# Hybrid attention block on one core: keys and values of units 4 to 15 as seven products of quarters, and head results kept in device memory until their gates

## The chip, the cores and the metric

The kernel runs on one core of a Trainium2 chip. The core has five engines, each with a queue of its own that it works through in order: PE (TensorE, matrix products), DVE (VectorE), ACT (ScalarE), POOL (GpSimd) and SP (SyncE, which here only issues DMAs). Engines wait for each other through semaphores. The metric is the device time of one execution in microseconds; 734.61 is the median of three runs before the change (734.28 to 734.91).

## What is computed

One decoder block on 512 tokens with 16 meta tokens in front (528 rows), 1024 channels, all in float32. Eight differential heads and sixteen stick-breaking heads, each branch with a SiLU gate:

```python
h = layer_norm(concat([meta, x]), emb_ln_g, emb_ln_b)             # 528 x 1024
q_d,k_d,v_d,g_d, q_s,k_s,v_s,g_s, m_d,m_s = split(h @ w_in)       # 10 x 1024 columns
a   = softmax(q1 k1' + alibi) - lam * softmax(q2 k2' + alibi)     # differential, 8 heads
y_d = rms_norm(a @ v_d, diff_subln_g) * (1 - lam_init)
y_s = stick_breaking(q_s, k_s) @ v_s                              # 16 heads
br_d = (y_d * silu(g_d)) @ w_br_diff
br_s = (y_s * silu(g_s)) @ w_br_sb
merged = sigmoid(m_d + b0) * br_d + sigmoid(m_s + b1) * br_s
out = layer_norm(DN_ALPHA * h + merged @ w_out, ln_g, ln_b)[16:]
```

## The kernel before

**Three passes.** h stands transposed in SBUF, channels on partitions, as eight k-tiles of 128 channels by 528 columns. It is held as a rounded part `hTh` and the rest `hTl` (L348), and every weight tile is split in the same way: `wh` by a cast on ACT (L153), `wl` by a subtraction on DVE (L158). A product is wh·hTh + wh·hTl + wl·hTh, three matmuls per k-tile.

**Weights.** They come as halves of four k-tiles (128 x 4 x 128, 256 KB). `items` and `loads` (L83 to L99) list them in the order of use; `fetch` (L118) issues the loads on SP into a ring `raw` of six, and `prep(h)` (L162) casts and splits half h and goes on fetching. It is called four halves ahead of the product that uses it. Where an item is a pair, `add` (L135) forms the sum of two halves on DVE, and where a load has a second source, POOL issues a DMA that adds it to the first in SBUF (L129).

**Units.** `UNITS` holds eight differential heads (kind d), then eight pairs of stick-breaking heads (kind s). Iteration u of the main loop runs the attention of unit u in steps between the projections of later units: keys (`stage_k`, L540) and values (`stage_v`, L567) of unit u+1, the query (`stage_q`, L527) of unit u+2, and, in s units, the two gates of that pair index. Keys and values run in `proj_pos` (L453): 8 k-tiles x 3 passes x 2 halves of 264 columns, 48 matmuls each, 96 a unit (L462). Query and gates run in `proj_tok` (L439): 24 matmuls of 512 columns. `stage_k` splits its result into `ks` (ACT L555, DVE L556), and `store_k` (L559) copies it into the one K buffer of each head by SP DMAs, as a step at 9.2 in the middle of the iteration; `stage_v` copies its result into `vT` on ACT (L574). `values` (L577) transposes vT on PE (tv, L582; the 16 meta rows t4, L586). PSUM has three banks for projections (`pj`).

**Order.** `run` interleaves the projection generators with attention steps at given times, and a scheduler then orders the middle of the program on each engine by its own estimate. `keep_order` (L192) pins the order of the start only. Everything between may move.

**Results.** d heads end in `ydT[:, h, :]` (L748), s pairs in `ysT`, two tiles of 16 KB a partition that live until the gates have been multiplied in (`gate`, L470, on POOL) and the branch products read them.

**Late stage.** The branch products already use seven products of quarters instead of eight (`pair`, L872, L886, 256 columns), on sums of quarters formed by `operands` (L853) and of weight quarters.

## Time and profile before

| what | value |
|---|---|
| median of three runs | 734.61 us (734.28 to 734.91) |
| profiled execution | 734.92 us |
| its span | 733.1 us, 13328 instructions |
| mean granted clock of PE | 0.994 |
| PE, DVE, ACT, POOL busy | 719.2, 529.9, 411.1, 176.6 us |
| DMA moved | 84.03 MB, mean 115 GB/s |

A group of instructions in the profile reads: line, engine, operation, output<-inputs, sizes, count | busy us in all, mean ns of one | idle us of the engine ahead of them and what ended it. A row of the timeline reads: start us, duration us, engine, line, operation, and in brackets the idle time before it with the instruction that ended it. Matmuls overlap in the array: one of 264 columns is listed with 0.28 us, while the next starts earlier.

### The profile page before, as it was taken

The numbers are of one execution on the slowest core, as the hardware profiler recorded it, in microseconds if no ns is written. First come the engines' busy times: TensorE is split into PE (matmuls) and PEld (weight loads), VectorE is DVE, ScalarE is ACT, GpSimd is POOL, SyncE is SP. The second block draws the span as 40 slices with busy tenths as digits, with TensorE's granted clock in tenths as the row PEclk, the third lists the DMA queues.
The fourth block names the chain that finished last, engine by engine and source line by source line (L and its number), as shares of the span: only waits on it lengthen the run. The fifth ranks groups of instructions, "written<-read, shape, count | busy, mean of one in ns | idle before, by whom it ended". The sixth has DMA issues, their size and how long they took to land.

```text
span 733.1 us, 13328 instructions
## 1 busy us (share of the span) xinstructions
PE 719.2 (98%) x4690; PEld 659.4 (90%) x4690; DVE 529.9 (72%) x1098; ACT 411.1 (56%) x987; POOL 176.6 (24%) x241
## 2 busy tenths in 40 slices
PE   8999999999999999999999999999999999999994
PEld 7999999999999989898989898988888998999883
DVE  6776667666766688585858585858385878788887
ACT  5675667566756756564646464646364456555300
POOL 3232244224412213120303030313022201230002
PEclk9999999999999999999999999999999999999997
DMA  9153443334323334232323333332248837696902
GB/s 292 37 145 101 104 117 91 89 99 117 93 83 102 95 95 113 77 104 75 106 81 100 90 95 94 89 88 71 73 114 156 170 109 185 135 185 186 313 17 101
DMA packets 134788, 84.03 MB, mean 115 GB/s; under 512 B 6161, under 2 KB 128434, under 8 KB 134722
## 3 DMA queue, kind: packets, MB, share of 16 engines
q1 hardware_dynamic: 125090, 76.36, 36.4%
q0 software_dynamic: 9312, 5.77, 5.9%
q10 hardware_dynamic: 320, 1.06, 0.4%
q8 instruction: 37, 0.61, 0.3%
q14 instruction: 29, 0.24, 0.1%
HBM read 67.32 MB, written 2.10 MB: 95 GB/s over the span
## 4 chain that ended last, share of the span: by engine, by line
PE 88%; DVE 6%; DMA 3%; POOL 1%; issue 1%; ACT 1%; SPq 0%; POOLq 0%; ACTq 0%; DVEq 0%
PE ps L462 25%; PE ps L448 12%; PE ps L446 11%; PE ps L447 11%; PE q L886 10%; PE sc L615 6%; PE t L621 4%; PE t L626 1%; DMA lgb<-in_ln_b_dram 1%; PE bank L337 1%; PE av L783 1%; PE tv L582 1%; PE av L784 1%; DVE hr L1035 1%; DMA raw<-in_w_out_dram 1%
## 5 line engine op out<-in xcount | busy, mean ns | idle before, releaser
L158 DVE TENSOR_TENSOR wl<-raw,wh 128x512 fp32r<-128x512 f32 x180 | 125.5, 704 | 93.9 <-ACT wh L153 85.8
L153 ACT CAST wh<-raw 128x512 fp32r<-128x512 f32 x180 | 110.8, 622 | 75.3 <-PE ps L447 62.0
L462 PE MATMUL ps<-hTh,wh 128*128 128x264 f32 x512 | 146.9, 287 | 0.0
L462 PE MATMUL ps<-hTl,wh 128*128 128x264 f32 x512 | 146.5, 286 | 0.0
L462 PE MATMUL ps<-hTh,wl 128*128 128x264 f32 x512 | 146.4, 286 | 0.0
L447 PE MATMUL ps<-hTl,wh 128*128 128x512 f32 x368 | 145.0, 394 | 0.0
L448 PE MATMUL ps<-hTh,wl 128*128 128x512 f32 x368 | 144.7, 393 | 0.0
L446 PE MATMUL ps<-hTh,wh 128*128 128x512 f32 x368 | 144.4, 393 | 0.0
L462 PEld LDWEIGHTS ps<-hTh,wh 128*128 128x128 f32 x512 | 96.5, 188 | 1.0
L462 PEld LDWEIGHTS ps<-hTl,wh 128*128 128x128 f32 x512 | 96.5, 188 | 1.0
L462 PEld LDWEIGHTS ps<-hTh,wl 128*128 128x128 f32 x512 | 96.5, 189 | 0.3
L448 PEld LDWEIGHTS ps<-hTh,wl 128*128 128x128 f32 x368 | 69.2, 188 | 13.1
L446 PEld LDWEIGHTS ps<-hTh,wh 128*128 128x128 f32 x368 | 69.2, 188 | 13.0
L447 PEld LDWEIGHTS ps<-hTl,wh 128*128 128x128 f32 x368 | 69.2, 188 | 12.5
L615 PE MATMUL sc<-k,A 128*128 128x264 f32 (+3 forms) x320 | 68.5, 298 | 0.2 <-POOL k L525 0.2
L769 DVE TENSOR_TENSOR_SCAN e<-e,after 128x528 f32<-128x528 f32 (+1 forms) x64 | 55.9, 883 | 13.2 <-ACT e L761 12.8
L886 PE MATMUL q<-gh,wh 128*128 128x256 f32 x224 | 63.5, 283 | 0.2 <-ACT t L895 0.2
L767 POOL TENSOR_SCALAR_AFFINE_SELECT e<-e 128x128 f32<-128x128 f32 x64 | 38.7, 612 | 103.3 <-ACT e L763 94.6
L886 PE MATMUL q<-gl,wh 128*128 128x256 f32 x224 | 63.4, 283 | 0.0
L886 PE MATMUL q<-gh,wl 128*128 128x256 f32 x224 | 63.4, 283 | 0.0
L707 POOL TENSOR_SCALAR e<-e,rz 128x528 f32<-128x528 f32 (+3 forms) x32 | 38.4, 1200 | 100.2 <-DVE rz L706 100.2
L631 ACT CAST ah<-t 128x512 fp32r<-128x512 f32 (+2 forms) x88 | 39.4, 464 | 37.0 <-PE t L621 30.6
(239 smaller groups left out, 1419.2 us busy)
## 6 DMA issues: line engine op xcount, KB each, us to landing
raw<-in_w_in_dram SPq DMA_DIRECT2D x152, 256.0 KB, 3.0
k<-ks SPq DMA_DIRECT2D x60, 132.0 KB, 2.6
raw<-in_w_out_dram SPq DMA_DIRECT2D x16, 256.0 KB, 3.3
k<-ks SPq DMA_DIRECT2D x60, 66.0 KB, 2.0
raw<-in_w_br_diff_dram SPq DMA_DIRECT2D x12, 256.0 KB, 3.0
raw<-in_w_br_sb_dram SPq DMA_DIRECT2D x12, 256.0 KB, 3.7
raw<-in_w_in_dram SPq DMA_DIRECT2D x4, 512.0 KB, 6.2
rawa<-in_w_br_diff_dram SPq DMA_DIRECT2D x8, 256.0 KB, 4.5
```

The costliest lines, as they stand in the source:

```text
L153: s.copy(wh, raw)
L158: eng.tensor_tensor(wl, raw, wh.bitcast(F32), op=ALU.subtract)
L446: pe.matmul(ps, wh[:, k % 4, :], hTh[:, k, M:], start=(k == 0), stop=False)
L447: pe.matmul(ps, wh[:, k % 4, :], hTl[:, k, M:], start=False, stop=False)
L448: pe.matmul(ps, wl[:, k % 4, :], hTh[:, k, M:], start=False, stop=(k == KT - 1))
L462: pe.matmul(ps[:, :H2], a[:, k % 4, :], b[:, k, ts(c, H2)], start=(k == 0 and m == 0), stop=(k == KT - 1 and m == 2))
L615: pe.matmul(ps[:, :n], q, K[:, m, k0:k0 + n], start=(m == 0), stop=(m == 1))
L631: s.copy(h, t[:, o:o + w])
L707: g.tensor_scalar(e[0], e[0], r[:, 0:1], None, op0=ALU.mult)
L767: g.affine_select(own, own, pattern=[[-1, P]], compare_op=ALU.is_gt, fill=0.0, base=0, channel_multiplier=1)
L769: v.tensor_tensor_scan(rev, rev, after[0][:, L - nk:][:, ::-1], 1.0, ALU.mult, ALU.max)
L886: pe.matmul(bank, a[:, k, :], b[:, n, k, :], start=start and k == 0 and m == 0, stop=k == 3 and m == 2, skip_group_check=not start)
```

## The change

From unit 4 on (`SEVEN = 4`, 12 of 16 units), `stage_kv` takes the place of `stage_k` and `stage_v`. It sees keys and values as one product of 2 x 2 quarters: weights by (key or value) and (first or last four k-tiles), h by (first or last four k-tiles) and (positions 0 to 263 or 264 to 527). Strassen's scheme in Winograd's form gives the four result quarters from seven products of 12 matmuls (4 k-tiles x 3 passes), 84 a unit. The line numbers from here on are those of the changed kernel.

It needs sums of weight quarters: per unit two of the five loads get a second source by an accumulating DMA of POOL (ring `rawk` of 4), and two more sums are formed by `add` on DVE. There are seven items a unit to cast and split, where there were four halves. It also needs four sums of quarters of h, made once: `input_sums(k)` for four pairs of k-tiles, into `tS` (rounded) and four tiles `tl` (rest). For that the float h (`hF`) is kept in pair tiles, its 16 meta columns apart in `hM`. Since the `tS` and `tl` tiles take the room of `ysT` and `ydT`, the results wait in device memory: a d head's `yd` is stored there (L827), an s unit loads it back for its gate, `gate` stores both gated results (L493), and the last unit reloads them. `store_k` is called at the end of `stage_kv` instead of by a step. The ring of sums has one buffer instead of two.

```diff
+SEVEN = 4
...
-            seq += [(x + UNITS[u + 1][0], UNITS[u + 1][1]) for x in "kv"]
+            other, i = UNITS[u + 1]
+            seq += [(x + other, i) for x in ("w" if u + 1 >= SEVEN else "kv")]
...
-            loads += [(a11, None), (a21, a11), (a21, a22), (a12, None), (a22, None)]
+            loads += [(a11, None, "raw"), (a21, a11, ring), (a21, a22, ring), (a12, None, "raw"), (a22, None, "raw")]
...
-    rings = {False: ("raw", 6, []), True: ("rawa", 4, [])}
+    rings = {"raw": (6, []), "rawk": (4, []), "rawa": (4, [])}
...
-    hF = ypool.tile([P, KT, L], F32, tag="yd", name="hF")
+    hP = [pair_of("hF") for k in range(4)]
+    hF = [hP[k % 4][:, k // 4, :] for k in range(KT)]
+    hM = const.tile([P, KT, M], F32, name="hM")
...
-        g.tensor_tensor(y[:, j, :], sg, y[:, j, :], op=ALU.mult)
+        y = y()
+        g.tensor_tensor(y, sg, y, op=ALU.mult)
+        if store is not None:
+            nc.sync.dma_start(store, y)
...
+        def input_sums(k):
+            g.tensor_copy(hP[k][:, :, :M], hM[:, k:k + 5:4])
+            b11, b12, b21, b22 = [hP[k][:, m, ts(n, H2)] for m in range(2) for n in range(2)]
+            v.tensor_tensor(b22, b12, b22, op=ALU.subtract)
+            v.tensor_tensor(b12, b11, b12, op=ALU.subtract)
+            v.tensor_tensor(b11, b22, b11, op=ALU.subtract)
+            v.tensor_tensor(b21, b11, b21, op=ALU.add)
+            h, l = tS[0][:, k:k + 5:4], pair_of("tl", F32R)
+            s.copy(h, hP[k])
+            v.tensor_tensor(l, hP[k], h.bitcast(F32), op=ALU.subtract)
+            tL.append(l)
+
+        def stage_kv(unit, kind, n):
+            i = take("w" + kind, n, 7)
+            x, z, y = [pj.tile([P, 512], F32, tag="pj", name="q")[:, :H2] for m in range(3)]
...
+            yield from product(0, x, 0)
+            s.copy(u, x)
+            yield from product(1, z, 5)
+            s.copy(z7, z)
+            yield from product(2, x, 4, False)
+            s.copy(w, x)
+            yield from product(3, y, 1)
+            v.tensor_tensor(u, y, u, op=ALU.add)
+            keys(0, u)
+            yield from product(4, x, 3, False)
+            v.tensor_tensor(vT[:, H2:], z7, x, op=ALU.subtract)
+            yield from product(5, z, 6, False)
+            v.tensor_tensor(vT[:, :H2], z, w, op=ALU.subtract)
+            unit["vT"] = vT
+            yield from product(6, x, 2, False)
+            keys(1, x)
+            store_k()
...
-            v.scalar_tensor_tensor(ydT[:, h, :], av, g08, r, op0=ALU.mult, op1=ALU.mult)
+            y = gpool.tile([P, S], F32, tag="sg", name="yd")
+            v.scalar_tensor_tensor(y, av, g08, r, op0=ALU.mult, op1=ALU.mult)
+            nc.sync.dma_start(kept["d"][h], y)
...
         def keys_values(unit, kind, n):
+            if UNITS.index((kind, n)) >= SEVEN:
+                return [stage_kv(unit, kind, n)]
             return [stage_k(unit, kind, n), stage_v(unit, kind, n)]
...
-            if not last:
-                steps.append((10.6 if kind == 's' and n == 0 else 9.2, store_k))
+            if u + 1 < SEVEN:
+                steps.append((9.2, store_k))
+            if u + 4 in (SEVEN + 1, SEVEN + 2):
...
+                for m in range(2):
+                    steps.append((5.0 + 6.0 * m, lambda k=2 * (u + 3 - SEVEN) + m: input_sums(k)))
...
                 if last:
...
+                    nc.sync.dma_start(ydT[7], kept["d"][7])
+                    for y, of in ((ydT, "gd"), (ysT, "gs")):
+                        for j in range(7):
+                            nc.sync.dma_start(y[j], kept[of][j])
...
+                    yd, unit["y"] = [gpool.tile([P, S], F32, tag="sg", name=x) for x in ("yd", "ys")]
+                    nc.sync.dma_start(yd, kept["d"][n])
+                    proj += [gate("d", n, lambda yd=yd: yd, kept["gd"][n]),
+                             gate("s", n, lambda unit=unit: unit["y"], kept["gs"][n])]
```

`input_sums` is written as steps of iterations u = 1 and u = 2. Where the scheduler puts it shows on DVE in the opening, between the copies of unit 0's second half of K (`ps_453`, `ps_484`) and the first low weight half of unit 1 (`wl_520`). Before, DVE has this there:

```order
L551 TENSOR_TENSOR k1_450<-ps_453,k1_450 64x264
L312 SCALAR_TENSOR_TENSOR A0_172<-bank_181,A0_172 64x512
L312 SCALAR_TENSOR_TENSOR A1_173<-bank_181,A1_173 64x512
L551 TENSOR_TENSOR k0_449<-ps_484,k0_449 64x264
L551 TENSOR_TENSOR k1_450<-ps_484,k1_450 64x264
L698 ISA e0_447,mn_618<-sc_621,bias_612 128x264
L698 ISA mn_618 128x1
L158 TENSOR_TENSOR wl_520<-raw_119,wh_519 128x512
```

After the change, in the stretch that ends with the same half (`wl_550`; the banks are `ps_483` and `ps_514`), it reads:

```order
L568 TENSOR_TENSOR k1_456<-ps_483,k1_456 64x264
L602 TENSOR_TENSOR hF_177<-hF_177 128x264
L602 TENSOR_TENSOR hF_178<-hF_178 128x264
L602 TENSOR_TENSOR hF_179<-hF_179 128x264
L605 TENSOR_TENSOR tl_1094<-hF_176,tS_956 128x1056
L319 SCALAR_TENSOR_TENSOR A0_174<-bank_187,A0_174 64x512
L319 SCALAR_TENSOR_TENSOR A1_175<-bank_187,A1_175 64x512
L568 TENSOR_TENSOR k0_455<-ps_514,k0_455 64x264
L605 TENSOR_TENSOR tl_1222<-hF_177,tS_956 128x1056
L605 TENSOR_TENSOR tl_1453<-hF_178,tS_956 128x1056
L568 TENSOR_TENSOR k1_456<-ps_514,k1_456 64x264
L605 TENSOR_TENSOR tl_1573<-hF_179,tS_956 128x1056
```

All four `input_sums` have moved up into the opening; the other thirteen of their sixteen 128x264 operations stand above these rows, among the first copies of K, and behind them come one score and `wl_550`. On ACT the casts into `tS` (L604) stand between the copies of K in the same stretch, ahead of `wh_549`, the high half that goes with it:

```order
L567 CAST k0_455<-ps_514 64x264
L604 CAST tS_956<-hF_177 128x2x528
L604 CAST tS_956<-hF_178 128x2x528
L604 CAST tS_956<-hF_179 128x2x528
L569 CAST k0_455<-ps_514 64x264
L567 CAST k1_456<-ps_514 64x264
L569 CAST k1_456<-ps_514 64x264
L160 CAST wh_549<-raw_121 128x512
```

Before, the four copies of that half of K (L550 and L552) stand there one behind the other with `wh_519` next; only the three casts are new among them.

The second place is PE in a d unit, around the transposition t4 of the meta rows of the unit's own values. Before:

```order
L725 MATMUL av_2546<-al0_2494,V_2274 128x512
L726 MATMUL av_2546<-ah0_2493,V_2274 128x512
L586 MATMUL t4_2604<-idents_127,vT_2382 16x128
L615 MATMUL sc_2703<-k0_449,A0_2238 128x272 x2
L462 MATMUL ps_2712<-hTh_148,wh_2479 128x264
L462 MATMUL ps_2712<-hTl_149,wh_2479 128x264
```

After, at the corresponding transposition (`q_2683` is the bank x of `stage_kv`):

```order
L802 MATMUL av_2656<-al0_2609,V_2373 128x512
L803 MATMUL av_2656<-ah0_2608,V_2373 128x512
L663 MATMUL t4_2715<-idents_129,vT_2345 16x128
L692 MATMUL sc_2852<-k1_456,A1_2337 128x272 x2
L692 MATMUL sc_2867<-k0_455,A0_2336 128x144 x2
L626 MATMUL q_2683<-hTh_150,wh_2770 128x264
```

The 24 matmuls of the query projection (`ps_2933`, L459 to L461) now stand ahead of these rows, with ten matmuls on `av` between; the seventh product, which adds to bank x after DVE has read that bank for vT, is now the last projection of the unit. Before, key and value matmuls stood behind t4 and the query projection followed them. On DVE that read (L646) stands here, behind the query's A0 and one `apad`:

```order
L165 TENSOR_TENSOR wl_3029<-rawk_2505,wh_3028 128x512
L552 SCALAR_TENSOR_TENSOR A0_3018<-ps_2933,A0_3018 64x512
L786 SCALAR_TENSOR_TENSOR apad0_433<-e1_454,rz_2698,e0_453 128x400
L646 TENSOR_TENSOR vT_2686<-kvt_1662,q_2683 128x264
L648 TENSOR_TENSOR vT_2686<-q_2684,kvt_1662 128x264
```

Before, vT was written by a copy of ACT (L574), and no matmul of the keys and values waited for it.

105 lines of the change are left out of this document (71 added, 34 removed).

## The prediction

> **What bounds the kernel now.** The page's shares of the span, the granted clock in 40 slices and the chain that ended last are read first.
>
> ```profile
> PE 719.2 (98%) x4690; PEld 659.4 (90%) x4690; DVE 529.9 (72%) x1098; ACT 411.1 (56%) x987; POOL 176.6 (24%) x241
> ...
> PEclk9999999999999999999999999999999999999997
> ...
> PE 88%; DVE 6%; DMA 3%; POOL 1%; issue 1%; ACT 1%; SPq 0%; POOLq 0%; ACTq 0%; DVEq 0%
> PE ps L462 25%; PE ps L448 12%; PE ps L446 11%; PE ps L447 11%; PE q L886 10%; PE sc L615 6%; PE t L621 4%; PE t L626 1%; DMA lgb<-in_ln_b_dram 1%; PE bank L337 1%; PE av L783 1%; PE tv L582 1%; PE av L784 1%; DVE hr L1035 1%; DMA raw<-in_w_out_dram 1%
> ```
>
> TensorE is busy 98% of 733.1 us at an undiminished clock, and a quarter of the chain is L462, the keys and values that the change rewrites. The view of waits, for TensorE, holds nothing but this:
>
> ```profile
> PE warm L267 <- POOL idents masks.py:199: 1.5, 1, 1.5
> PE bank L300 <- DVE xn L296: 0.9, 1, 0.9
> PE bank L300 <- ACT cols L362: 0.2, 1, 0.2
> PE q L886 <- ACT t L895: 0.2, 1, 0.2
> PE sc L615 <- POOL k L525: 0.2, 1, 0.2
> ```
>
> That is 3.0 us in all, 2.6 of it in the opening. From the first unit on TensorE waits for nobody, so a matmul taken out there is worth its full spacing until some other engine comes late. How near the others are, the windows show (start:end, length, then busy time with count of PE, PEld, DVE, ACT, POOL, then clock, DMA share, GB/s).
>
> ```profile
> 29.20:38.60 9.40, 9.24 (x76) 9.03 (x75) 4.96 (x11) 4.70 (x12) 7.01 (x19) 1.00 0.01 3
> ...
> 102.45:126.81 24.36, 24.36 (x176) 23.07 (x174) 16.50 (x48) 16.06 (x43) 9.10 (x11) 1.00 0.40 107
> ...
> 255.00:289.00 34.00, 34.00 (x232) 31.55 (x231) 31.16 (x52) 22.39 (x61) 10.47 (x14) 1.00 0.34 93
> ...
> 420.25:436.00 15.75, 15.75 (x131) 15.73 (x130) 13.30 (x22) 11.51 (x32) 6.34 (x8) 1.00 0.27 79
> 436.00:457.50 21.50, 21.50 (x111) 18.19 (x111) 12.63 (x26) 9.53 (x22) 1.91 (x3) 1.00 0.37 103
> ```
>
> A differential unit lasts 24.36 us with VectorE busy 16.50. A stick-breaking unit lasts 37.25 us: 15.75 of keys and values with VectorE at 84%, then 21.50 of query and gates with VectorE at 59%. From 255 to 289 VectorE is 92% busy and TensorE still loses nothing.
>
> **What is saved.** Each of the 12 changed units runs 7 products of 12 matmuls, 84, where L462 ran 96: 12 fewer a unit, 144 in all, with the same 264 columns. Their spacing is read from start to start:
>
> ```profile
> 33.57 0.29 PE L462 MATMUL ps<-hTl,wh 128*128 128x264 f32 x1
> 33.69 0.28 PE L462 MATMUL ps<-hTh,wl 128*128 128x264 f32 x1
> 33.81 0.28 PE L462 MATMUL ps<-hTh,wh 128*128 128x264 f32 x1
> ```
>
> 0.12 us (0.28 is the pipelined length). L462's share of the chain gives the same: 25% of 733.1 over 1536 matmuls is 0.119. At a median spacing of 0.121, 144 are 17.4 us, or 1.45 us a unit. [...] The seven-product scheme already runs in the late stage (L886), where the only wait is the 0.2 us above, so the scheme in itself starves nothing.
>
> **What it costs at the start.** The scheduler has placed all four `input_sums` into the opening, ahead of the low weight halves of unit 1. That is 16 VectorE operations of 128x264, four of 128x1056, and four ScalarE casts of 128x1056. The nearest rows:
>
> ```profile
> L348 DVE TENSOR_TENSOR hTl<-hF,hTh 128x256 fp32r<-128x256 f32 x16 | 5.6, 418 | 0.0
> L868 DVE TENSOR_TENSOR gl<-t,gh 128x1024 fp32r<-128x1024 f32 x8 | 9.8, 1226 | 1.5 <-ACT gh L867 1.5
> L867 ACT CAST gh<-t 128x1024 fp32r<-128x1024 f32 x8 | 8.4, 1055 | 13.0 <-DVE t L864 13.0
> ...
> 25.00 2.77 DVE L348 TENSOR_TENSOR hTl<-hF,hTh 128x256 fp32r<-128x256 f32 x8
> ```
>
> Eight subtractions of 256 columns in 2.77 us are 0.346 apiece; times 264/256 that is 0.357, and 16 take 5.7 us. A 128x1056 takes 1.226 x 1056/1024 = 1.26 alone, some 1.2 in a row; four take 4.8. Together **10.5 us of VectorE**. What room is there? Between 29.2 and 38.6 VectorE is busy 4.96 of 9.40 us (window above): 4.4 idle, all of it waiting for ScalarE's copies.
>
> ```profile
> 34.54 1.39 DVE L312 SCALAR_TENSOR_TENSOR A<-bank,A 64x512 fp32r<-64x512 f32 x2 [1.66 <-ACT A L307]
> ...
> 38.63 1.90 DVE L158 TENSOR_TENSOR wl<-raw,wh 128x512 fp32r<-128x512 f32 x3 [0.49 <-ACT wh L153]
> ...
> 39.94 0.28 PE L462 MATMUL ps<-hTh,wl 128*128 128x264 f32 x1
> ```
>
> The first wl is ready at 38.63 + 0.69 = 39.3 and used at 39.94, a slack of 0.6. So 10.5 - 4.4 - 0.6 = 5.5. Walking the copies, sums and casts in their new order, with ScalarE's casts of 1.05 standing between the copies of K, the first key matmul that needs wl starts at 45.5 instead of 39.94: **5.6 us**. Full durations instead of spacings give 7.6; the low end is 0, if the scores and values can be moved so that TensorE has work meanwhile, but its row holds only unit 0's 48 value matmuls (5.8 us) before them, as before. Nothing later gives this back, since TensorE is the bound afterwards. GpSimd can add to it:
>
> ```profile
> 150.02 1.64 POOL L683 TENSOR_SCALAR bias<-bias 128x528 f32<-128x528 f32 x1 [0.46 <-DVE mn L698]
> ...
> 150.18 1.11 DVE L158 TENSOR_TENSOR wl<-raw,wh 128x512 fp32r<-128x512 f32 x1
> ```
>
> A wl of 0.69 takes 1.11 us beside a 1.64 us bias on POOL; two such biases run in the opening, so up to 0.8 more, which I keep in the upper end. [...]
>
> **What it costs in the differential units** (five of them work on units 5 to 9 of the 16). Prices:
>
> ```profile
> L158 DVE TENSOR_TENSOR wl<-raw,wh 128x512 fp32r<-128x512 f32 x180 | 125.5, 704 | 93.9 <-ACT wh L153 85.8 <-PE av L785 6.9
> L153 ACT CAST wh<-raw 128x512 fp32r<-128x512 f32 x180 | 110.8, 622 | 75.3 <-PE ps L447 62.0 <-PE ps L462 10.4 <-PE q L886 1.6
> L535 DVE SCALAR_TENSOR_TENSOR A<-ps,A 64x512 fp32r<-64x512 f32 x28 | 19.3, 688 | 1.9 <-ACT A L534 1.1
> L534 ACT ACTIVATE A<-ps 64x512 fp32r<-64x512 f32 x28 | 16.6, 592 | 4.4 <-DVE A L535 3.6
> L556 DVE TENSOR_TENSOR ks<-ps,ks 128x264 fp32r<-128x264 f32 x30 | 12.8, 426 | 3.6 <-ACT ks L555 3.3
> L140 DVE TENSOR_TENSOR sum<-rawa,raw 128x512 f32<-128x512 f32 x8 | 5.5, 684 | 0.0
> L709 DVE SCALAR_TENSOR_TENSOR apad<-e,rz,e 128x400 f32<-128x400 f32 x8 | 5.8, 728 | 0.0
> ...
> 175.53 0.39 PE L446 MATMUL ps<-hTh,wh 128*128 128x512 f32 x1
> ...
> 178.28 0.39 PE L446 MATMUL ps<-hTh,wh 128*128 128x512 f32 x1
> ```
>
> Seven weight halves instead of four are 3 x 0.70, two sums 2 x 0.68, and u, and the two vT halves that leave ScalarE, 3 x 0.43: 4.75 us more VectorE a unit, 21.25 of 22.9 us (24.36 - 1.45), or 93%. ScalarE gains three casts of 0.6 and about one copy, some 2.2 us, of a third that is idle. The share says it fits; the order says where it doesn't. The last product adds to the bank from which vT (L646) is read, so TensorE waits for that read. Behind the last query matmul VectorE's row has A0 (after ScalarE's A), apad 128x400, then vT: 0.39 (the matmul's end behind its start) + 0.59 + 0.69 + 0.73 + 0.43 = 2.8, some 2.6 with VectorE's overlap of successive operations. TensorE has ten matmuls on `av`, t4 and two pairs of scores in that time: 3328 + 128 + 832 columns at 0.447 ns (twelve of 512 columns start in the 2.75 us from 175.53 to 178.28, 0.229 each), with the query matmul's own 0.23, 2.1 us. That leaves 0.5 us a unit, **2.7 us** over five (2.5 by this sum, rounded up for a queue at 93%); the ends are 0, if the query's A comes earlier, and 1.2 each.
>
> **What it costs in the stick-breaking units** (seven). 4.75 us on 25.9 gives 30.7 of 35.8, 86%. Within the 14.3 us that remain of the keys and values 13.30 + 4.75 would be too much, but the order has part of the products stand among the query and gate matmuls, where VectorE has 8.9 us idle. Walked waits keep 1.3 to 1.5 us of slack; I take 0.17 each, **1.2 us**, with ends 0 and 3.75 each (18.05 - 14.3).
>
> **What is hidden.** The results kept in device memory and reloaded are loads of 256 KB under a DMA share of 0.4 or less; POOL's two accumulating loads a unit occupy a quarter-used engine.
>
> ```profile
> rawa<-in_w_br_diff_dram SPq DMA_DIRECT2D x8, 256.0 KB, 4.5
> rawa<-in_w_br_diff_dram POOLq DMA_DIRECT2D x8, 256.0 KB, 6.2
> k<-ks SPq DMA_DIRECT2D x60, 132.0 KB, 2.6
> ```
>
> An accumulation lands 6.2 us after its issue, behind a 4.5 us plain load; the ring of four is fetched a whole unit ahead, so I cost it at nothing. If that cover failed, a unit would lose up to 6.2. SP waits a few microseconds where a result isn't finished; six buffered weight halves hold some 16 us of TensorE's work. The last unit's 15 reloads wait on the release of the operands tS and tl, with gates in between: nothing. K's second half is stored right behind the last product, and has about 0.4 us to spare on a landing of 2.6.
>
> **The sum**, against the profiled execution's 734.92 (span 733.1 and 1.8 around it; the median shown is 734.61): 734.9 - 17.4 + 5.6 + 2.7 + 1.2 = **727.0 us**. A measurement of this kernel can tell about 0.2% from no change, so faster is below 733.1 and slower above 736.1.
>
> **The rivals.** (a) *The covers hold*: the opening overlaps and VectorE keeps up. For it: TensorE lost nothing at 92% VectorE. Against it: the order at the start. 734.9 - 17.4 = 717.5, with a stall or two 718. (b) *Slower: VectorE becomes the bound of the stick-breaking units' keys and values.* If nothing moved into the gates' time, 3.75 x 7 = 26 us on top of the 5.6 and 2.7: 752; with half of it, 741. It decides from a loss of 17.4/12 = 1.45 us a unit, opening included. Against it: the order does spread the products. (c) *K's halves land late*, 0.5 to 1.2 us in 12 units: 727 + 6 to 14, 733 to 741, near no change. For it: 0.4 us of slack; against it: stores of 2.6 us were never waited for before. (d) *A clock drop after the opening's stall*: the trace shows the clock at 1.00 in the opening window, but also no gap there as long as the 3 us now to come. Were half the clock granted for some 4 us behind it, 2 to 3 us of work would be lost: 730. [...]
>
> **How the numbers follow.** Forecast (725 to 731) 0.50; (a) 0.18; (b) 0.13; (c) 0.12; (d) 0.07. Its own range follows from 5.6 to 7.6 at the start, 0 to 1.2 in five units and 0 to 0.3 in seven. The range that leaves out (b) alone, and a little of (c), goes from 717 to 737. Faster: 0.50 + 0.18 + 0.07 + part of (c), 0.80; same 0.06; slower, (b) and the rest of (c), 0.14.
>
> **What would show it.** L626 with 1008 matmuls at 0.12 spacing and 384 left to the old line confirms the saving. The first key matmul of unit 1 near 45.5, behind VectorE's hF and tl rows, confirms the opening; near 40 refutes it. Waits of TensorE on vT L646, five of about 0.5, confirm the differential units; waits on wl or sums of over a microsecond in the stick-breaking units mean (b), on k<-ks (c), a PEclk digit under 9 in the second slice or third (d). The forecast is wrong if VectorE's order under load makes one late operation queue behind the next, so that stalls add up unit by unit.

## The result, and the profile after

| | before | after |
|---|---|---|
| median, beside each other on one chip | 734.76 us (734.28 to 736.24, 4 runs) | 746.78 us (745.65 to 747.76, 4 runs) |
| profiled span | 733.1 us | 744.7 us |
| mean granted clock of PE | 0.994 | 0.983 |

The ratio is 1.016, with a 95% interval of 1.0138 to 1.0181: the changed kernel is **slower by 12.0 us**, where 727.0 was forecast, and it lies outside the range. The page of the changed kernel first: busy shares, granted clock in 40 slices, the chain by engine.

```profile
PE 716.7 (96%) x4546; PEld 651.2 (87%) x4546; DVE 597.4 (80%) x1214; ACT 441.2 (59%) x1043; POOL 212.3 (29%) x269
...
PEclk9989999999999998999999999999999999999998
...
PE 80%; DVE 7%; DMA 4%; POOL 3%; issue 3%; ACT 3%; SPq 0%; ACTq 0%; DVEq 0%; POOLq 0%
```

TensorE runs 144 matmuls less (4690 to 4546), as forecast, but its share of the chain falls from 88% to 80%, and POOL, which had 1%, now has 3%. Two slices have an 8 in the clock where there was a 9. The view of waits says for whom TensorE waits (us in all, times, longest):

```profile
PE q L626 <- DVE vT L646: 6.1, 4, 2.4
PE av L863 <- DVE al L709: 3.6, 1, 3.6
PE ps L475 <- ACT k L569: 2.5, 1, 2.5
PE sc L692 <- ACT e L842: 2.3, 1, 2.3
...
PE sc L692 <- POOL k L542: 1.2, 1, 1.2
...
PE sc L692 <- DMA k<-ks: 0.2, 1, 0.2
```

Where they lie, the windows show (start:end, length, then busy time with count of PE, PEld, DVE, ACT, POOL, then clock, DMA share, GB/s). First the changed kernel:

```profile
20.00:40.00 20.00, 16.30 (x114) 15.37 (x113) 19.47 (x54) 13.18 (x34) 9.08 (x26) 0.91 0.36 79
...
100.00:240.00 140.00, 133.26 (x907) 124.08 (x906) 115.74 (x297) 98.09 (x254) 63.20 (x70) 0.99 0.58 135
240.00:300.00 60.00, 53.21 (x322) 47.68 (x321) 45.51 (x78) 44.04 (x99) 19.32 (x26) 0.91 0.48 121
...
380.00:540.00 160.00, 159.87 (x958) 141.71 (x958) 129.13 (x228) 95.83 (x240) 35.05 (x45) 1.00 0.49 139
```

The same stretches of the kernel before:

```profile
100.00:240.00 140.00, 140.00 (x993) 132.48 (x993) 93.93 (x256) 92.14 (x240) 47.27 (x65) 1.00 0.36 97
240.00:300.00 60.00, 60.00 (x383) 54.29 (x382) 46.06 (x80) 38.95 (x95) 13.18 (x18) 1.00 0.35 98
```

There TensorE was busy throughout. Now it is idle for 3.7 us in the opening, for 6.7 in the differential units and for 6.8 at the passage to the stick-breaking units; from 300 us on it loses next to nothing.

The same loss by spacing: I take the time from a matmul's start to the next one's start, subtract the median for its size, and add up what is over 0.15 us. Beside it stands what the matmuls lose while the clock is at one half (left out: the first 20 us, where the first 128x128 matmuls of both kernels stand 0.21 us apart, up to 4.2 us before and 5.7 after, and the next ones 0.11).

| stretch, us | before | after: stalls | after: half clock |
|---|---|---|---|
| 20 to 60 (opening) | 0.5 | 4.5 | 2.5 |
| 60 to 240 (differential units) | 0.0 | 7.7 | 1.6 |
| 240 to 300 (passage) | 0.0 | 9.4 | 3.8 |
| 300 to the end | 0.4 | 1.4 | 0 |

That is 23.0 + 7.9 us lost, against 0.9 before; less the 17.4 saved it makes 12.6, where the spans differ by 11.6. Some 1.4 us stand in both columns: at the passage, matmuls of 512 columns that the clock slows lose over 0.15 us each and count as stalls too.

The saving itself is there. The groups of TensorE by form (count, then busy us and mean ns of one):

```profile
L626 PE MATMUL q<-tS,wh 128*128 128x264 f32 x192 | 56.0, 292 | 0.8 <-DVE A L552 0.7
...
L626 PE MATMUL q<-hTh,wh 128*128 128x264 f32 x144 | 42.8, 297 | 6.1 <-DVE vT L646 6.1
...
L475 PE MATMUL ps<-hTh,wh 128*128 128x264 f32 x128 | 38.3, 299 | 2.5 <-ACT k L569 2.5
```

Three forms of 192 and three of 144 are 1008 matmuls on L626, and 3 x 128 = 384 stay on the old line, as forecast.

**One stall followed back.** The timeline of the changed kernel around the first long wait on vT, POOL, VectorE and TensorE one below the other (start, duration; in brackets the idle time before and what ended it):

```profile
178.56 1.28 POOL L136 DMA_DIRECT2D rawk<-in_w_in_dram  x1 [5.45 <-DMA rawk<-in_w_in_dram]
179.35 2.14 POOL L784 TENSOR_SCALAR e<-e,rz 128x528 f32<-128x528 f32 x1
180.94 0.72 POOL L785 TENSOR_TENSOR rz<-rz,nlam 128x1 f32<-128x1 f32 x1
...
176.06 0.16 DVE L783 RECIPROCAL rz<-zs 128x2 f32<-128x2 f32 x1
...
181.69 0.77 DVE L786 SCALAR_TENSOR_TENSOR apad<-e,rz,e 128x528 f32<-128x528 f32 x1 [2.43 <-POOL rz L785]
...
185.49 0.43 DVE L646 TENSOR_TENSOR vT<-kvt,q 128x264 f32<-128x264 f32 x1
...
185.97 0.39 PE L626 MATMUL q<-hTh,wh 128*128 128x264 f32 x1 [2.40 <-DVE vT L646]
```

POOL had the accumulating load next in its queue and waited 5.45 us for the plain load that it adds to. The reciprocal that the scaling of e (L784) needs was ready at 176.22, but L784 stands behind that DMA and starts at 179.35. So VectorE waits 2.43 us for rz, forms apad late, comes to A and then to vT late, and TensorE waits 2.40 us. The forecast had half a microsecond at this place.

### The profile page after: what moved, and what is told of

It reads as the page before. It is cut to its first block, busy times and chain, and to the rows that moved or that the text cites. A ratio compares the mean times of both kernels' runs of the same rounds, so it can differ in the third digit from the quotient of the medians.

```text
span 744.7 us, 13453 instructions
## 1 busy us (share of the span) xinstructions
PE 716.7 (96%) x4546; PEld 651.2 (87%) x4546; DVE 597.4 (80%) x1214; ACT 441.2 (59%) x1043; POOL 212.3 (29%) x269
## 4 chain that ended last, share of the span: by engine, by line
PE 80%; DVE 7%; DMA 4%; POOL 3%; issue 3%; ACT 3%; SPq 0%; ACTq 0%; DVEq 0%; POOLq 0%
PE q L626 15%; PE ps L460 11%; PE ps L459 11%; PE ps L461 11%; PE q L985 9%; PE ps L475 6%; PE sc L692 5%; PE t L698 3%; DMA lgb<-in_ln_b_dram 1%; PE t L703 1%; DMA rawk<-in_w_in_dram 1%; PE bank L350 1%; PE av L862 1%; PE av L863 1%; POOL e L784 1%
## 5 line engine op out<-in xcount | busy, mean ns | idle before, releaser
L459 PE MATMUL ps<-hTh,wh 128*128 128x512 f32 x368 | 145.8, 396 | 0.0
L461 PE MATMUL ps<-hTh,wl 128*128 128x512 f32 x368 | 145.3, 395 | 0.0
L160 ACT CAST wh<-raw 128x512 fp32r<-128x512 f32 x168 | 102.9, 621 | 35.5 <-PE ps L460 20.6
L461 PEld LDWEIGHTS ps<-hTh,wl 128*128 128x128 f32 x368 | 69.6, 189 | 12.9
L459 PEld LDWEIGHTS ps<-hTh,wh 128*128 128x128 f32 x368 | 69.6, 189 | 12.8
L460 PEld LDWEIGHTS ps<-hTl,wh 128*128 128x128 f32 x368 | 69.6, 189 | 12.1
L784 POOL TENSOR_SCALAR e<-e,rz 128x528 f32<-128x528 f32 (+3 forms) x32 | 46.1, 1441 | 56.9 <-DVE rz L783 56.9
L136 POOL DMA_DIRECT2D rawk<-in_w_in_dram x24 | 32.4, 1381 | 99.5 <-DMA rawk<-in_w_in_dram 62.2
L709 DVE TENSOR_TENSOR al<-t,ah 128x512 fp32r<-128x512 f32 (+2 forms) x88 | 45.7, 525 | 18.4 <-ACT ah L708 11.2
L692 PEld LDWEIGHTS sc<-k,A 128*128 128x128 f32 x320 | 51.4, 192 | 9.2 <-ACT e L842 2.7
L626 PE MATMUL q<-tS,wh 128*128 128x264 f32 x192 | 56.0, 292 | 0.8 <-DVE A L552 0.7
L626 PE MATMUL q<-tl,wh 128*128 128x264 f32 x192 | 55.4, 289 | 0.0
L626 PE MATMUL q<-tS,wl 128*128 128x264 f32 x192 | 55.0, 288 | 0.0
```

The source lines that it names most:

```text
L160: s.copy(wh, raw)
L459: pe.matmul(ps, wh[:, k % 4, :], hTh[:, k, M:], start=(k == 0), stop=False)
L460: pe.matmul(ps, wh[:, k % 4, :], hTl[:, k, M:], start=False, stop=False)
L461: pe.matmul(ps, wl[:, k % 4, :], hTh[:, k, M:], start=False, stop=(k == KT - 1))
L626: pe.matmul(bank, a[:, k, :], b, start=start and k == 0 and j == 0, stop=k == 3 and j == 2, skip_group_check=not start)
L692: pe.matmul(ps[:, :n], q, K[:, m, k0:k0 + n], start=(m == 0), stop=(m == 1))
```

## The experiments

Each time stands beside the kernel before on the same chip.

| run | what it is | median us | ratio to before (95%) |
|---|---|---|---|
| e1_sums | after, sums of the input out of the opening | 740.79 | 1.008 (1.006 to 1.011) |
| e5_park | results parked in device memory, no seven products | 736.82 | 1.002 (1.000 to 1.004) |
| e9_noacc | e1 without the accumulating loads | 728.69 | 0.991 (0.990 to 0.993) |
| e8_noadd | e1 without VectorE's weight sums | 732.95 | 0.997 (0.995 to 0.999) |
| e10_both | e1 without either | 728.64 | 0.989 (0.986 to 0.992) |
| e2_pool | after, accumulations issued three halves later | 760.68 | 1.036 (1.034 to 1.038) |
| e11_window | e1, accumulations at a fixed step | 750.96 | 1.020 (1.017 to 1.023) |
| e13_early | e1, accumulations a unit earlier | 741.04 | 1.007 (1.005 to 1.010) |
| e12_junk | e9 and 24 accumulations into spare memory | 741.91 | 1.009 (1.006 to 1.013) |
| e14_plain | e9 and 24 copies by SP | 729.49 | 0.992 (0.990 to 0.994) |
| e17_work | e9 and 24 x 1.3 us of POOL's time | 728.93 | 0.991 (0.989 to 0.992) |
| e19_pinned | e1 in e9's order | 749.78 | 1.022 (1.019 to 1.025) |
| e3_tables | after, ScalarE's table loads grouped | 753.56 | 1.025 (1.022 to 1.027) |
| e4_all | e1, e2 and e3 together | 757.76 | 1.032 (1.030 to 1.034) |
| e7_s9 | seven products from unit 9 on | 734.70 | 0.999 (0.998 to 1.000) |
| e15_s11 | from unit 11 on, table loads grouped | 728.56 | 0.990 (0.989 to 0.992) |
| e16_s11n | from unit 11 on | 728.50 | 0.991 (0.989 to 0.992) |
| e18_s10 | from unit 10 on | 727.49 | 0.989 (0.987 to 0.991) |

### The opening, and the results in device memory

`place()` ties an instruction behind the one that was written before it on the same engine, so that the scheduler can't draw the sums into the opening.

```diff
             v.tensor_tensor(b22, b12, b22, op=ALU.subtract)
+            place()
             v.tensor_tensor(b12, b11, b12, op=ALU.subtract)
+            place()
```

> One edit to the changed kernel: the first two VectorE operations of each input_sums are ordered behind the VectorE instruction that the program issues before them, so that the sums stay in iterations 1 and 2 instead of the opening. If the opening's loss comes from them (the ms matmul of unit 0 stands 6.9 us later than before, that of unit 1 6.3), they start within 1 us of before and the time falls by about 6 us to some 741. Rival: the 10.5 us of VectorE only move into units that are nearly full, and the time stays at 744 to 747.

740.79 against 746.78: 6.0 us, where the forecast had 5.6 for this step. The stalls between 20 and 60 us fall from 4.5 to 0.6. But the wait was not the forecast's. The changed kernel's timeline, ScalarE and TensorE:

```profile
35.75 1.07 ACT L604 CAST tS<-hF 128x1056 fp32r<-128x1056 f32 x1 [1.33 <-POOL bias L757]
36.73 0.37 ACT L569 CAST k<-ps 64x264 fp32r<-64x264 f32 x1
...
34.12 0.48 PE L692 MATMUL sc<-k,A 128*128 128x264 f32 x2 [1.16 <-POOL k L542]
37.15 0.59 PE L475 MATMUL ps<-hTh,wh 128*128 128x264 f32 x1 [2.55 <-ACT k L569]
...
45.92 0.28 PE L475 MATMUL ps<-hTh,wh 128*128 128x264 f32 x1
```

TensorE waited not for wl but earlier, for POOL's clearing of k and for ScalarE's part of unit 0's keys (L569), which stands behind a cast of the sums (L604). Then it ran 26 matmuls at a spacing of 0.22 instead of 0.12, at half clock (2.5 us). The first matmul of unit 1's keys starts at 45.92, where the forecast had 45.5 for the first one with wl: the size was right by luck, since another sum gave it. With the sums moved, the units lose as before (10.8 us of stalls from 60 to 240), so this is one part only.

The other cheap part: seven products off altogether, results still parked.

```diff
-SEVEN = 4
+SEVEN = 16
...
-            if u + 4 in (SEVEN + 1, SEVEN + 2):
+            if SEVEN < 16 and u + 4 in (SEVEN + 1, SEVEN + 2):
```

> The changed kernel with SEVEN at 16 and without input_sums: no unit uses the seven products, but heads' results still wait in device memory, hF stands in pair tiles and the sum ring has one buffer. Theory: parking is hidden, within 1.5 us of before (733.5 to 736.5), TensorE waits under 4 us. Rival: the parking's stores and reloads, or the order that they bring, cost a part of the loss in the units; then 738 or more.

1.5 us above before, at the edge of what can be told (the interval includes no change). There is no stall in the units, so there the parking is hidden, as forecast; the two stalls over 0.35 us, 1.0 and 0.9, lie at 671 and 675 us, in the branch products.

### The loads that were costed at nothing

Left out here: the second source of 24 weight quarters, so that the products of units 4 to 15 work on other weights. All else is done as in e1_sums.

```diff
-            if more is not None:
+            if more is not None and tag != "rawk":
                 g.dma_start(raw, more, accum_op=ALU.add)
```

> e1_sums without POOL's accumulating loads in the units (the plain load stands for the sum; this leaves computation and 24 x 256 KB of loads out): VectorE has the same work. Theory of POOL's queue: the stalls between 100 and 380 us fall by half or more, 733 or less, and POOL's scaling of e goes back from 1.44 to 1.2 us. Theory of the full VectorE: at most 3 us, 738 to 741.

12.1 us less than e1_sums. What is left on vT then, in that kernel's view of waits:

```profile
PE q L636 <- DVE vT L656: 1.7, 4, 0.6
```

Four waits of up to 0.6 us are the forecast's differential units (0.5 each). So that sum is about right for a kernel without these loads. VectorE's two weight sums a unit are the other relief that I tried, alone and together with this one (they are left out of the computation, and one of the two weight quarters stands in for the sum):

```diff
-        v.tensor_tensor(raw, one, raws[second], op=ALU.add)
+        if whole:
+            v.tensor_tensor(raw, one, raws[second], op=ALU.add)
+        elif first is not None:
+            raw = one
...
-            add(h + 1)
+            add(h + 1, names[h + 1][0][0] != "w")
```

> e1_sums without VectorE's two sums of weight quarters per unit (the first summand stands for the sum; this leaves computation out): VectorE 1.37 us lighter in each changed unit, 20 instead of 21.3 of 22.9 in a differential one. Theory of the full VectorE: of the some 17 us of stalls between 100 and 380 us at least half goes, 740.8 - 8 = 733 or less. Rival (POOL's accumulating loads or the loads themselves): within 2 us of e1's 740.8.

> e1_sums without POOL's accumulating loads in the units and without VectorE's two sums of weight quarters (computation left out, as in e8 and e9 together). If the two reliefs stand for one cause (the attention's chain through VectorE and POOL is late), they don't add: 726 to 729. If they are separate, 740.8 - 7.8 - 12.1 = 721, with 17.4 saved nearly whole.

7.8 us for the sums alone, 12.1 for the loads alone, 12.2 for both by the medians, and some 14 by the ratios, since the chip of e10_both was slower: the reliefs don't add. That both act on one chain, POOL's scaling and VectorE's row behind it, would explain it; no run shows that by itself.

**Is it POOL's waiting?** The accumulation adds to its plain load, and POOL waits until that one has landed. The changed kernel's view of POOL's waits has this row:

```profile
POOL rawk L136 <- DMA rawk<-in_w_in_dram: 62.2, 9, 10.9
```

So I had the issue wait until three more halves had been prepared.

```diff
-                g.dma_start(raw, more, accum_op=ALU.add)
+                owed.append((state["n"] + LATE, l, raw, more))
...
+            g.dma_start(raw, more, accum_op=ALU.add)
+            place()
```

> One edit to the changed kernel: an accumulating load is issued on POOL three weight halves later than its plain load, and ordered behind the POOL instruction that the program issues before it. If POOL's in-order queue is the cause of the late units (it stands waiting for the plain load with the scaling of e behind it), POOL's idle time at the rawk issue falls from 62 us to under 10, the wait of 3.6 us on al L709 at 283.5 goes, the vT waits fall from 6.1 us to the 2.5 or less of the forecast, and the time falls by 7 to 9 us to some 739. Rival: VectorE is too full by itself; the vT waits stay near 6 us and the time at 745 to 747.

A miss: 760.68. POOL no longer waits for rawk, but now others do, in that kernel's waits of ScalarE and of VectorE:

```profile
ACT wh L173 <- DMA rawk<-in_w_in_dram: 15.9, 6, 5.2
```

```profile
DVE sum L158 <- DMA rawk<-in_w_in_dram: 11.8, 7, 3.5
```

The two loads stand one behind the other, 3.4 and 5.2 us in the DMA issues of the changed kernel's page, and the cast has to come behind both. Issued early, in the changed kernel, the second held up POOL (62.2 us); issued late, here, it held up the cast (15.9 us) and the sums (11.8). Moving the whole pair earlier might be the way out, and two kernels tried it: both fetch `rawk` out of turn (16 and 24 loads ahead) and issue the accumulations at step 12 of each iteration; the second has a ring of six for `rawk` and of four for `raw`.

```diff
+            steps.append((12.0, lambda: [pay(owed[0][1]) for _ in range(len(owed))]))
             run(proj, steps)
...
-    rings = {"raw": (6, []), "rawk": (4, []), "rawa": (4, [])}
+    rings = {"raw": (4, []), "rawk": (6, []), "rawa": (4, [])}
```

> e1_sums with all its work, but the weight quarters for the accumulating loads are fetched a whole unit ahead (as soon as the ring of four has room, not in their place in the list), and POOL's accumulations are issued together in the middle of each iteration, when POOL stands idle and the plain loads have landed. No engine waits for a landing then, while POOL issues the same 24 accumulations. If e9's gain of 12 us came from waiting (POOL on the plain load, and what is queued behind it), it comes here too: 728 to 731, faster than before by over 0.5%. If it came from the issue time on POOL or the traffic, the time stays at 738 to 741.

> e1_sums with all its work, with rings of 6 instead of 4 for the weight quarters that get a second summand and 4 instead of 6 for the other raw halves (same memory), so that a plain load and its accumulation come a unit earlier than in e11; POOL issues the two accumulations of a unit together in its idle stretch, and the late stage's accumulations stay where the changed kernel has them. Theory (an accumulated quarter lands just before its use, and the in-order engines behind it wait): no wait of DVE or ACT on rawk, 728 to 732 and faster than before. Rival (issue time or traffic): 737 or more. If the smaller ring of raw halves hurts, it shows as waits on raw in the late stage.

The median of e11_window tells little, since my edit put off the branch weights' accumulations too, which cost about 12 us after 656 us. In e13_early the late stage loses about 5 us of stall and clock at 672 to 679, perhaps to the shorter `raw` ring, and its median of 741.04 is e1's. But in both POOL's waits on the loads of `rawk` are gone (in e11_window VectorE waits 9.8 us for them instead, in e13_early no engine does), and the units are little better for it: from 60 to 300 us the stalls are 16.6 us in e11_window and 14.7 in e13_early, against 17.3 in e1_sums and 8.3 in e9_noacc. POOL's waiting alone is not what the loads cost.

**POOL's time, the traffic, or the order?** Three kernels take e9_noacc and put something back that nobody waits for: accumulations of the same bytes into spare device memory; the same bytes copied by SP; 13 memsets of POOL in place of each accumulation.

```diff
-                g.dma_start(raw, more, accum_op=ALU.add)
+                g.dma_start(spare() if tag == "rawk" else raw, more, accum_op=ALU.add)
...
+                    nc.sync.dma_start(spare(), more)
...
+                    for _ in range(13):
+                        g.memset(idle, 0.0)
+                        place()
```

> e9_noacc with 24 accumulating loads of the same size issued by POOL all the same, two together in the middle of POOL's chain for the attention, but into spare device memory that nobody reads: POOL's issue time and the traffic of the weights are back, no engine waits for a plain load or for a landing (the sums are left out). If the landings were the cause of e9's 12 us, the time stays at 729 to 732; if POOL's issue time (2.6 us a unit ahead of the scaling of e) or the traffic, it goes back to 737 to 741.

> Left out of the computation: the second source of the weight quarters in units 4 to 15 is not added in. In place of each of these 24 accumulating loads of POOL, SP copies the same 256 KB into a spare piece of device memory, which nobody waits for. With the accumulations simply left out the kernel took 728.7 us; with 24 accumulations by POOL into spare memory 741.9. If it is POOL's time at the issue (1.3 us each in its queue, ahead of work that VectorE waits for) and the order that it makes, plain copies by SP cost little: 729 to 731, few stalls in units 4 to 9, no k<-ks waits. If it is the traffic or the landing of the K copies behind it, the time stays near 742, with k<-ks waits of about 6 us.

> Left out of the computation: the second source of the weight quarters in units 4 to 15 is not added in. In place of each of the 24 accumulating loads POOL does thirteen memsets of 128x8, about 0.1 us each and 1.3 together, most of them where the accumulations into spare memory stood; there is no DMA. If it is POOL's time in the middle of the attention's chain that costs, the time is 737 to 742, as with the accumulations into spare memory (741.9), and POOL's scaling of e comes late for VectorE. If it is the software DMA traffic (as K copies of 132 KB that land late), it is 728 to 731 without k<-ks waits, as with the copies by SP (729.5).

e12_junk comes to 741.91, 13.2 us above e9_noacc, though its loads wait for nothing and nobody waits for them. The longest wait of its TensorE is on the K copies:

```profile
PE sc L709 <- DMA k<-ks: 6.0, 3, 2.7
```

e14_plain is inconclusive: one row of its timeline shows that the scheduler put all 24 copies into the opening, so they were no traffic of the units.

```profile
18.55 22.17 SPq L142 DMA_DIRECT2D spare<-in_w_in_dram  x24
```

e17_work answers for POOL's time. Its group of memsets:

```profile
L139 POOL MEMSET idle<- 128x8 f32 x312 | 32.4, 104 | 15.6
```

32.4 us, the very sum of the changed kernel's 24 accumulations (32.4), stand close to e12's accumulations (a block at 174.45 us where two of e12's stand at 176.17, and so on unit by unit), and cost 0.2 us. Occupying POOL with memsets is free in these places; so the forecast's "quarter-used engine" was right as far as it went.

But e17's TensorE also has, but for a swapped pair, the order of e9 (VectorE and ScalarE nearly so), while in e12 another row stands at 504 of TensorE's 4546 places. With a DMA of POOL in the program the scheduler makes another order. Is the order the loss? The last kernel is the whole computation with every instruction, apart from the 24 accumulations, tied to its place in e9:

```diff
+        ranks = []
+        for run_ in PINNED[eng.name].split():
+            a, _, n = run_.partition("+")
+            ranks += range(int(a), int(a) + int(n or 1))
+        for a, b in zip(ranks, ranks[1:]):
+            follow(row[b], row[a])
```

> The whole computation, with all 24 accumulating loads of POOL. Every instruction of TensorE, VectorE, ScalarE, SP and (apart from these 24) POOL is pinned to the place that it had in the version without the accumulations (728.7 us). If the accumulations cost their time on the chip (a late landing, POOL's issue, their traffic), the time stays at 737 to 745, with waits on DMA rawk, or on ScalarE and VectorE behind it, as in the other orders. If the loss was in the order that the scheduler makes of the other engines' work once these loads are in the program, the time is 728 to 732, with the same few stalls as without them (231 to 250, 280, 322).

749.78: in the same order, the loads cost **21.1 us** (e9_noacc 728.69), 15.5 of it stalls by the measure above and most of the rest at half clock. So they cost time without any change of order; left to itself the scheduler makes room for them and gets by with 12.1. The waits of TensorE in e19_pinned:

```profile
PE q L737 <- DVE vT L757: 7.5, 5, 3.2
...
PE sc L803 <- DVE mn L886: 3.0, 1, 3.0
```

and its timeline at two of them:

```profile
34.53 4.14 POOL L235 DMA_DIRECT2D rawk<-in_w_in_dram  x3 [0.16 <-issue]
...
38.23 2.36 POOL L235 DMA_DIRECT2D rawk<-in_w_in_dram  x1
39.42 4.40 POOL L871 TENSOR_SCALAR bias<-bias 128x528 f32<-128x528 f32 x2
...
42.24 0.43 DVE L886 CUSTOM_DVE_ANT_0 e<-sc,bias 128x264 f32<-128x264 f32 x1 [4.45 <-POOL bias L871]
...
178.20 1.34 POOL L235 DMA_DIRECT2D rawk<-in_w_in_dram  x1 [10.91 <-DMA rawk<-in_w_in_dram]
...
181.41 0.77 DVE L897 SCALAR_TENSOR_TENSOR apad<-e,rz,e 128x528 f32<-128x528 f32 x1 [1.31 <-POOL rz L896]
...
185.26 0.39 PE L737 MATMUL q<-hTh,wh 128*128 128x264 f32 x1 [1.35 <-DVE vT L757]
```

At both, what VectorE waits for is an operation of POOL (the bias, rz) that stands behind an accumulating load in POOL's queue. But only at the second did the load wait for another load, for 10.91 us, with rz behind it. At the first, four were issued between 34.53 and 40.59 us, with 0.16 us of idle time ahead of them: there the issue itself holds up the bias, and TensorE for 3.0 us. None of e17's memsets stands at this place.

The rows show one more effect, which the waits don't. Here are one row of VectorE in e19_pinned, and the same one in e9_noacc:

```profile
163.56 3.08 DVE L266 TENSOR_TENSOR wl<-raw,wh 128x512 fp32r<-128x512 f32 x1
...
156.51 0.81 DVE L165 TENSOR_TENSOR wl<-raw,wh 128x512 fp32r<-128x512 f32 x1 [0.64 <-PE sc L702]
```

In e19_pinned a load was issued at 163.43 us and two operations of POOL stand behind it. Seven rows of VectorE become over 1 us longer beside such a load or the operation of POOL right behind it, by 12.1 us together. VectorE's busy time rises from 590.8 to 601.2 us with the same operations in the same order; in e17_work, with memsets in place of the loads, it is 590.7.

So the loads are the cost, in any order, and three ways are seen in which they cost: the wait ahead of the issue, the issue where POOL is needed, and VectorE's longer rows beside it. How the 12.1 or 21.1 us divide among them isn't shown, nor what makes up e12_junk's 13.2 us: its other order, the issue, or the traffic beside the K copies.

### The passage to the stick-breaking units

In the changed kernel ScalarE loads its function tables in turn for exp, for the norm of the last differential head and for the stick-breaking scores: six loads of 1.28 us from 241 to 261 us, where the kernel before has three from 233 to 254. The first edit ties each kind together.

```diff
                     s.activation(e[c], e[c], AF.Exp, scale=-1.0, bias=m[:, 0:1], accum_out=zs[:, i, c:c + 1])
+                    behind("act", h == 7)
...
-            behind("act", h == 7)
+            behind("act", h >= 6)
```

> One edit to the changed kernel: on ScalarE the exponentials of differential head 7 and the logarithm and exponential of head 6's norm are ordered ahead of the first sigmoids of unit 8, so that three table loads stand there instead of six or seven. If the switching of tables is the cause of the gap of 2.5 us at 251 and of the half clock behind it, both go and the time falls by about 4 us to 743. Rival: the gap has its cause in VectorE or POOL and only moves; 746 to 747.

> The three edits of the runs before it together. If the three causes are separate and make up the loss, the gains add: 746.8 - 6 - 8 - 4 = 729, near the 727 that the prediction's sum gave, with TensorE waiting under 6 us in all. Rival: the waits are several that stand for one another (a full VectorE), so that the gains don't add and the time stays above 735.

Misses: the loads fall from six to three, but the times are 753.56 and, with all three edits, 757.76. The scheduler's new order brings other waits (the stalls from 240 to 300 us are 15.2 us in e3_tables, where the changed kernel has 9.4), and the edits don't add. So I looked at where seven products may stand at all.

```diff
-SEVEN = 4
+SEVEN = 9
...
-            if u + 4 in (SEVEN + 1, SEVEN + 2):
+            if u - 4 in range(4):
...
-                for m in range(2):
-                    steps.append((5.0 + 6.0 * m, lambda k=2 * (u + 3 - SEVEN) + m: input_sums(k)))
+                steps.append((8.0, lambda k=u - 4: input_sums(k)))
```

(The sums of the input come one apiece in four differential iterations. The same with 11 and 10 in place of 9; then the first of the four iterations is 6 or 5. Table loads are tied in e7_s9 and e15_s11 alone.)

> Seven products only for units 9 to 15, so that every differential iteration keeps its 96 matmuls; input_sums one apiece in iterations 4 to 7, ordered as in e1; tables ordered as in e3. Theory (a nearly full VectorE with a fixed order is what makes the differential units late): they lose at most 2 us, the seven changed units save 7 x 1.45 = 10.2, time 726 to 729. Rival (the seven products cost as much in any unit, through POOL, loads or tables): 733 or more.

> Seven products from unit 11 on (5 units, all of them behind the first two stick-breaking iterations), sums of the input made in the differential iterations 6 to 9, one apiece, table loads of ScalarE pinned. If the stick-breaking units from the tenth iteration on are clean, as in the run with nine, 5 x 1.45 = 7.3 us are saved and at most 1.5 given back for the sums and the results that wait: 728 to 730, ratio 0.991 to 0.994, no stall over 1 us at 240 to 290. If every order of this program loses several us somewhere, whatever the units, it stays at 733 to 737.

> The same from unit 11 on, without the pinning of ScalarE's table loads. If the transition to the stick-breaking units loses time only where the seven products run there, this gives the same 728 to 730; if the pinning itself costs or saves in the transition, the two differ by over 1.5 us with stalls at 235 to 260.

> Seven products from unit 10 on (6 units), sums of the input in iterations 5 to 8, ScalarE's table loads not pinned. One clean unit more than with eleven would give 1.45 us more, 727.1; but its products stand in iteration 9, beside the first stick-breaking heads, where the version with nine lost 8 us at 242 to 285: if the loss belongs to that iteration, 729 to 734 with stalls there.

From unit 9 on: no gain, with 9.3 us of stalls from 240 to 300. From unit 11 on: 728.5, with or without the tie, no stall over 0.4 us in the units. From unit 10 on: **727.49, ratio 0.989 (0.987 to 0.991)**, 8.3 us faster than before on its chip, where the change was 12.0 slower on its own, and with the whole computation. Its windows:

```profile
240.00:290.00 50.00, 50.00 (x324) 45.48 (x323) 43.26 (x75) 37.10 (x91) 15.16 (x20) 1.00 0.46 121
290.00:380.00 90.00, 90.00 (x554) 80.47 (x553) 75.29 (x137) 54.40 (x135) 24.12 (x27) 1.00 0.57 146
```

Six units give 6 x 1.45 = 8.7 us, and 8.3 are measured, with POOL's accumulations in place. There the scheme costs next to nothing.

Why unit 9 fails is seen best without the accumulations, in e9_noacc (ScalarE, then TensorE):

```profile
232.42 1.28 ACT L831 ACT_TABLE_LOAD   x1
233.71 0.69 ACT L831 ACTIVATE r<-ms,epsr 128x512 f32<-128x512 f32 x1
234.42 1.28 ACT L833 ACT_TABLE_LOAD   x1
...
236.76 0.37 ACT L651 COPY kvt<-q 128x264 f32<-128x264 f32 x1
...
237.18 0.39 PE L636 MATMUL q<-tS,wh 128*128 128x264 f32 x1 [1.78 <-ACT kvt L651]
```

In the iteration where the last differential head ends and the first stick-breaking heads begin, a copy out of PSUM, on which the next product waits, stands behind two table loads of 1.28 us. The old way of keys and values has no copy there on which TensorE waits at once. That the tables alone make the loss isn't shown: in e7_s9, with the loads tied, the waits at 244 to 284 are on VectorE's kvt and al.

## Why the prediction was wrong

**The saving**: right. 144 matmuls are gone; in the six units of e18_s10 they are worth what was forecast (8.3 of 8.7 us, sums and parking included).

**The opening, 5.6 us**: right in size (6.0 measured by e1_sums), but by luck: the wait was another (k of unit 0, then half clock) in place of wl.

**The differential units, 0.5 us each**: about right only for a kernel without the accumulating loads (up to 0.6, four times, in e9_noacc). In the changed kernel the four waits on vT are 6.1 us.

**What failed: "the ring of four is fetched a whole unit ahead, so I cost it at nothing".** The landing was looked at, and POOL's busy share, but not what stands *behind* the issue in POOL's queue, nor that POOL waits for the first load ahead of the issue (62.2 us in all), nor that rows of VectorE beside it get longer (seven in e19_pinned, by 12.1 us together). In place of nothing, the loads cost 12.1 us in e1_sums' own order and 21.1 in one made without them. How much of that each of the three effects makes stays open. The forecast named the sign of it among what would make it wrong ("one late operation queue behind the next"), but gave it no term.

**The passage** was not in the sum: the forecast priced the differential and the stick-breaking units, not the iteration between them. Against a forecast of 721.4 for e9_noacc (727.0 less the 5.6 of the opening, which it doesn't have), 7.3 us remain, by its stalls most of them between 230 and 325 us. So the 19.8 us between forecast and result are 0.4 of opening, 12.1 of loads, and a rest of 7.3, most of it at and behind the passage.

**The rivals.** (a), that the covers hold, fell with the result. (b), VectorE as the bound of the stick-breaking units, fell: 159.87 of 160 us busy from 380 to 540, with VectorE at 81%. (c), late halves of K, fell too: the longest such wait of the changed kernel is 0.2 us. (d), the clock, did happen, four times instead of once, and is worth 7.9 us, most of it within the parts above; its some 4 us at half clock were an assumption of mine, measured were 3.41 us twice and 6.83 us twice. No rival gave the accumulating loads a price; the one that forecast a slower kernel, (b), went by VectorE's share. **The parking**: right in the units (e5_park).

**Sums.** Two of the forecast's are off, without weight for the result: half of (b)'s 26 us gives 739, not 741, and the ends named for the forecast's own range give 723 to 733, not 725 to 731.

## What to carry to other kernels

Each accumulating load that POOL issued was an entry in POOL's queue here, with up to 10.9 us of waiting ahead of it in the changed kernel: of such a load ask what it waits for, what stands behind it and who works beside it, and not only how long it takes. 1.3 us of memsets in POOL's queue at each of 24 places cost 0.2 us in all, and as many loads cost 12 to 21 us. Of two loads in a row, one adding to the other, the second held up POOL when it was issued early (62.2 us in the changed kernel) and ScalarE's casts and VectorE's sums when it was issued late (15.9 and 11.8 us in e2_pool); moving both earlier took POOL's waits away here, but not the loss. And a saving that is sound in a steady unit need not hold in the iteration where one kind of unit turns into the next (9.3 us of stalls from 240 to 300 with seven products from unit 9 on, no wait over 0.2 us in the units with them from unit 10 on): leave that iteration as it is, as the version from unit 10 on does.

## What the runs showed of the hardware

In four stretches of the changed kernel, from 20 to 700 us, the granted clock was at a half, each at or behind one of TensorE's four longest waits. The windows around and behind these (2.55, with 1.16 shortly before it, then 2.40, 2.33 and 3.55 us):

```profile
38.00:43.00 5.00, 5.00 (x24) 5.00 (x24) 4.82 (x6) 4.35 (x7) 4.91 (x5) 0.50 1.25 156
186.00:190.00 4.00, 4.00 (x21) 4.00 (x22) 3.56 (x10) 2.70 (x8) 2.25 (x3) 0.58 0.19 56
254.00:258.00 4.00, 4.00 (x13) 3.13 (x13) 4.00 (x7) 3.24 (x10) 1.70 (x3) 0.61 0.15 45
288.00:292.00 4.00, 4.00 (x18) 3.79 (x18) 3.35 (x7) 2.92 (x7) 1.28 (x1) 0.50 0.42 132
```

Each costs some 1.5 to 2.5 us, as much again as many a stall. Behind waits of 1.68 us (to 212.42) and 1.49 us (to 237.16) the clock stayed at 1.00 in the same run (212 to 216, 236 to 240). The same wait of 1.78 us was followed by a clock of 0.64 in e17_work's 237 to 241 and by 1.00 in e9_noacc's 237.5 to 241, so the length alone doesn't decide.

The times at which the trace of the changed kernel has the clock change put it at a half from 36.46 to 43.29, 186.65 to 190.06, 254.91 to 258.32 and 285.63 to 292.46 us: twice 6.83 us and twice 3.41 (the first and the last begin while TensorE still waits). In the 3.41 us ahead of them TensorE was idle for 2.93, 2.40, 2.21 and 1.90 us. What decides beside the length of the wait is not shown.
